# Two RWKV steps at a time: state-free products taken out of the chain, next block's preparation first

## Chip, cores and metric

The kernel runs on one core of one Trainium2 chip. The metric is the device time of one execution in microseconds; the median of several runs counts.

## The reference

One layer of a hybrid diffusion block: 512 latent tokens and 256 context tokens of width 1024. An input projection feeds two head groups. The first is bidirectional RWKV-7 time mixing with 8 heads of 64; the second is bidirectional gated linear attention in chunks of 64. Both go through one output projection, a norm, and a mixture of 16 experts (1024 to 2816 to 1024), each of which takes its best 64 tokens. All is in f32. What the change touches is the RWKV recurrence, run over context and then latent tokens in each direction:

```python
def step(s, inp):
    r_t, w_t, kk_t, kka_t, k_t, v_t = inp
    s_kk = jnp.einsum('bhvk,bhk->bhv', s, kk_t)
    s = s * w_t[:, :, None, :] - s_kk[..., None] * kka_t[:, :, None, :] + v_t[..., None] * k_t[:, :, None, :]
    y = jnp.einsum('bhvk,bhk->bhv', s, r_t)
    return s, y
```

## The kernel before

The kernel first projects the inputs in strips, then runs the gated linear attention, then the RWKV part, then the output projection, norm and routing, and last the experts, whose weights are read from HBM in one pass.

The RWKV part works in chunks of 64 tokens: 4 of context and 8 of latent tokens, so 12 chunks a direction. Each chunk is solved with a triangular inverse, so that only a 64x64 state passes from chunk to chunk. The heads are taken in four blocks b of two heads each; both directions d run in the same step, on different chunks. For each block there are these stages.

- `rw_elem` makes the decays and rates from small matrices (tiles e_c, e_w, e_i, e_t, one buffer each), and PC, the decay over a whole chunk.
- `rw_keys` writes KB (keys and removal keys, side by side) and AM (decayed removal keys). AM holds the two heads in two halves, each half zero on the other head's partitions.
- `rw_scores` (L839) multiplies KB by AM for each chunk into the score matrices SC, masked by MA.
- `rw_inverse` inverts the triangular part of SC in place: a recursion of 15 pairs of VectorE operations (L881, L884), then diagonal 32x32 products (L896, L916, L919), then the off-diagonal corrections (L931 to L946).
- `rw_rho` writes RM, the decayed receptance, with the same zero halves.
- `rw_step`, twelve times: transposes values and keys (VU, kbt); multiplies scores by values into ps_w; adds AM by state S (L981); copies to wt (L984); multiplies by the inverse (L988); copies into VU (L992); multiplies keys by VU (L1000); and updates the state, S2 = PC * (product + S), with the part PC * S made on GpSimd (L1012, L1014). For the last eight steps `rw_out` makes the outputs from RM, S, KB and VU (L1025 to L1044).
- `rw_post` normalises the block's outputs and adds bonus and gate.

`rw_prep` is scores, inverse and rho together. The loop over b issues the steps of block b, then keys and preparation of block b+1, then the elements of block b+2, then the post of block b-1. Instructions are ordered by a scheduler that takes them by program order; `H(name, b)` moves a stage ahead by the number of places that OPT gives under that name (h_crit up to 1000, h_elem 700 for block 1, h_scores 700). PSUM has eight banks: w 1, k 2, e 2, i 2, u 1; the inversion uses i, elements, scores and post use e, the steps w, k and u. A few dummy matmuls (`busy`, and at L1361) run between stages. After the last block, `rows` (L1189) adds the output projection of three quarters of the heads for row tiles 1 and 2, and `begin` (L1200) starts the accumulation for each tile, with those products inside for tiles 0 and 3.

Of the kernel before, what the change touches and what calls it, by code (L numbers as in the profile page):

```python
# [15 lines left out]
OPT = dict(h_load=-100,h_rho=(0, 500, 60, 400),rh=(1, 2, 2, 2),b1=(0, 4),h_step=(0, 0, 0, 200),adb=4,h_post=(100, -100, 0),gf=512,h_rows=(0, 100),h_acc0=-100,h_scores=(500, 700, 0, -50),h_keys=(400, 500, 0, -100),b3=(0, 8),sp=1,gse='v',ea=1,f7=3,h_glah=0,bz=(10, 10),f3=1,r0b=0,fb=3,ge=0,p2=2,p1=0,f5=1,h_elem=(0, 700, 0, 60),f2=3,b2=(4, 0),h_inv=(200, 0, 0, 100),wo=(5, 6, 3, 4, 1, 2, 0, 8, 7),f8=3,f1=2,f6=1,h_split=0,f4=1,h_sub=(60, 60, 0, 150),h_out=(300, -100, 0, -200),h_crit=(700, 1000, 100, 400),vu='aa',h_lev=(150, 0, 0, 0),pwr=0,h_kv=(0, 0, 0, 0),h_post3=150)  # L16
# [6 lines left out]
P = 128  # L23
# [13 lines left out]
def body(tc, I, out):  # L37
# [91 lines left out]
    HR = (slice(0, 64), slice(64, 128))  # L129
    smask = pcn.tile([P, TT], BF16, name="smask")  # L130
# [541 lines left out]
    KB, AM, RM, SC = [[], []], [[], []], [[], []], [[], []]  # L672
    for n in "ct":
        rpa.tile([P, 2, TT], F32, name=f"e_{n}")
    for d in range(2):
        KB[0].append(rpa.tile([P, 12, P], F32, name=f"KB0{d}"))
        AM[0].append(rpa.tile([P, 12, 2, 64], F32, name=f"AM0{d}"))

    def rw_elem_(b, pss, fill=lambda n: None):
# [10 lines left out]
        PC = zp0.tile([P, 12, 2], F32, name="PC", bufs=2)  # L690
# [43 lines left out]
    def rw_keys_(b, PC, kk, c, ws, ips, tas):  # L734
        j = b % 2
        for d in range(2):
            V.tensor_tensor(KB[j][d][:, :, VR[d]], ch(c[d]), ch(ips[d]), op=M)
            V.tensor_tensor(KB[j][d][:, :, DR[d]], ch(tas[d]), ch(ips[d]), op=M)
            for h in range(2):
                r = HR[h]  # L740
                E = (G, V)[h]
                al, k3, w3 = AM[j][d][r, :, h], ch(kk)[r], ch(ws[d])[r]
                if d == 0:
                    E.tensor_tensor(al[:, :, 1:64], k3[:, :, 1:64], w3[:, :, 0:63], op=M)
                    G.tensor_copy(al[:, :, 0], k3[:, :, 0])
                else:
                    E.tensor_tensor(al[:, :, 0:63], k3[:, :, 0:63], w3[:, :, 1:64], op=M)
                    G.tensor_copy(al[:, :, 63], k3[:, :, 63])
# [5 lines left out]
    def rw_rho_(b, pss, PC, kk, c, ws, ips, tas):  # L754
        j = b % 2
        for d in range(2):
            for h in range(2):
                r = HR[h]
                G.tensor_tensor(RM[j][d][r, :, h], ch(zr[b])[r], ch(ws[d])[r, 4:12], op=M)
# [11 lines left out]
    def clear(j):  # L771

        for d in range(2):
            for h in range(2):
                G.memset(AM[j][d][HR[1 - h], :, h], 0.0)
# [34 lines left out]
    def pu_():  # L810
        return next(puq)
# [743 lines left out]
```

## Time and profile before

| | |
|---|---|
| median of 3 runs | 2114.52 us (2105.4 to 2122.06) |
| profiled execution | 2106.32 us |
| its span, first to last instruction | 2104.6 us |
| mean granted TensorE clock | 0.961 |
| TensorE busy | 1837.8 us (87%) |
| VectorE busy | 708.1 us (34%) |
| ScalarE busy | 482.8 us (23%) |
| GpSimd busy | 309.1 us (15%) |
| DMA moved | 638.58 MB |

A share of busy time is an average over stages with different limits, and a TensorE that is busy need not be at its peak, since products in flight count in full.

### The profile page before, as it was taken

The page shows a single profiled execution, that of the slowest core. Times are in us where ns is not written, and L with a number is a line of the kernel's source. Part 1 is how long each engine was busy: PE and PEld are TensorE (multiplying, and loading weights), DVE is VectorE, ACT ScalarE, POOL GpSimd, SP SyncE. Part 2 cuts the span into 40 slices and gives each one's busy share as a digit, 9 for nine tenths or more (in the row PEclk, how much of TensorE's full clock was granted, in tenths as well). Part 3 has the DMA queues.
Part 4 walks back from the last instruction along what each step waited for, and adds up shares of the span by engine and source line. Part 5 has one row for each costly group of instructions (what it writes and reads, how often), then busy time and mean ns, then how long its engine had stood idle before and what let it go on. Part 6 is the DMA issues. An engine that isn't in the chain of part 4 may idle for free. (4 is left out here: it accounts for less than half of the span.)

```text
span 2104.6 us, 32442 instructions
## 1 busy us (share of the span) xinstructions
PE 1837.8 (87%) x13882; PEld 941.6 (45%) x13882; DVE 708.1 (34%) x1381; ACT 482.8 (23%) x984; POOL 309.1 (15%) x317
## 2 busy tenths in 40 slices
PE   5999997788889988999998988988888888889886
PEld 1776776567667653333333333333333333333322
DVE  4233668666753262123112112122122121121113
ACT  2242445555752441011101100010010010011001
POOL 2442655343230220000000000000000000000001
PEclk9999998898987999999999999999999999999998
DMA  8457631510000268999999999999999999999995
GB/s 291 139 147 219 219 106 29 174 46 18 2 28 7 87 269 367 425 424 425 425 424 424 425 425 425 424 424 425 425 425 424 424 425 424 425 425 425 424 424 224
DMA packets 135996, 638.58 MB, mean 303 GB/s; under 512 B 13007, under 2 KB 73016, under 8 KB 84908
## 3 DMA queue, kind: packets, MB, share of 16 engines
q1 hardware_dynamic: 133520, 625.74, 73.6%
q0 software_dynamic: 2016, 10.49, 1.5%
q8 instruction: 109, 1.79, 0.4%
q10 hardware_dynamic: 316, 0.28, 0.1%
q14 instruction: 35, 0.29, 0.0%
HBM read 619.54 MB, written 15.75 MB: 302 GB/s over the span
## 5 line engine op out<-in xcount | busy, mean ns | idle before, releaser
L1443 PE MATMUL ps_gu<-wt,xT 128*64 128x512 f32 (+1 forms) x3072 | 689.3, 568 | 49.6 <-DMA wt<-in_ex_up_dram 36.9
L1443 PEld LDWEIGHTS ps_gu<-wt,xT 128*64 128x64 f32 x3072 | 239.7, 138 | 436.7 <-issue 292.0
L1491 PE MATMUL ps_gu<-wd,hT 128*64 128x512 f32 x1408 | 311.2, 595 | 30.6 <-DMA wd<-in_ex_down_dram 30.6
L1491 PEld LDWEIGHTS ps_gu<-wd,hT 128*64 128x64 f32 x1408 | 97.5, 137 | 232.4 <-issue 173.7
L1464 ACT ACTIVATE gT<-ps_m 128x512 f32<-128x512 f32 x16 | 9.6, 597 | 602.7 <-PE ps_m L45 602.7
L1505 DVE TENSOR_TENSOR ye<-ps_gu,g2b 128x512 f32<-128x512 f32 x16 | 11.1, 692 | 370.9 <-PE ps_gu L1491 370.9
L1406 PE MATMUL ps_m<-h,oh 128*64 128x512 f32 x256 | 93.2, 616 | 45.6 <-DVE oh L1401 45.6
L1294 POOL MEMSET cnt<- 128x12 f32 x16 | 1.7, 108 | 885.0 <-DVE rank L1316 873.0
L296 PE MATMUL ps_d<-hh,wh 128*128 128x512 f32 (+1 forms) x336 | 126.6, 377 | 4.5 <-ACT kx L356 3.1
L1517 DVE TENSOR_TENSOR kx<-kx,ps_m 128x512 f32<-128x512 f32 x120 | 77.1, 684 | 153.9 <-PE ps_m L1511 153.9
L296 PE MATMUL ps_d<-hh,wl 128*128 128x512 f32 (+1 forms) x336 | 121.7, 362 | 5.3 <-POOL wl L288 5.3
L296 PE MATMUL ps_d<-hl,wh 128*128 128x512 f32 (+1 forms) x336 | 122.3, 364 | 2.0 <-POOL hl L267 1.9
L1408 ACT ACTIVATE xg<-ps_m 128x512 f32<-128x512 f32 x16 | 9.6, 597 | 331.6 <-PE ps_m L1406 331.6
L288 POOL TENSOR_TENSOR wl<-raw,wh 128x1024 fp32r<-128x1024 f32 x26 | 65.3, 2512 | 108.1 <-ACT wh L287 90.9
L88 DVE TENSOR_SCALAR hm<-hm 128x512 f32<-128x512 f32 (+1 forms) x48 | 19.4, 405 | 179.1 <-ACT hm L1455 179.1
L296 PEld LDWEIGHTS ps_d<-hh,wh 128*128 128x128 f32 x336 | 65.4, 195 | 20.7 <-issue 6.7
L1415 DVE TENSOR_TENSOR xT<-ps_m,mod 128x512 f32<-128x512 f32 x16 | 11.1, 692 | 188.6 <-PE ps_m L1411 188.6
L296 PEld LDWEIGHTS ps_d<-hh,wl 128*128 128x128 f32 x336 | 65.7, 195 | 14.9 <-POOL wl L288 5.5
L296 PEld LDWEIGHTS ps_d<-hl,wh 128*128 128x128 f32 x336 | 65.6, 195 | 13.5 <-POOL hl L267 3.6
L1511 PE MATMUL ps_m<-ye,gT 64*128 64x512 f32 x244 | 68.8, 640 | 0.0
L1406 PEld LDWEIGHTS ps_m<-h,oh 128*64 128x64 f32 x256 | 28.9, 142 | 85.3 <-issue 77.7
L1300 DVE SCALAR_TENSOR_TENSOR scr<-ps_m,aff,lo 128x128 bf16<-128x128 f32 (+3 forms) x60 | 33.0, 551 | 93.0 <-PE ps_m L1396 91.4
(451 smaller groups left out, 2620.8 us busy)
## 6 DMA issues: line engine op xcount, KB each, us to landing
wt<-in_ex_gate_dram SPq DMA_DIRECT2D x128, 1408.0 KB, 26.4
wt<-in_ex_up_dram SPq DMA_DIRECT2D x128, 1408.0 KB, 27.0
wd<-in_ex_down_dram SPq DMA_DIRECT2D x96, 1536.0 KB, 27.6
wd<-in_ex_down_dram SPq DMA_DIRECT2D x32, 1024.0 KB
adat<-in_ada_w_dram SPq DMA_DIRECT2D x64, 256.0 KB, 3.6
raw<-in_w_in_dram SPq DMA_DIRECT2D x25, 512.0 KB, 5.7
adat<-in_ada_w_dram SPq DMA_DIRECT2D x4, 2048.0 KB
wo_d<-wx SPq DMA_DIRECT2D x16, 512.0 KB, 3.3
```

The costliest lines, as they stand in the source:

```text
L88: V.tensor_scalar(o, o, 1.0, 2.0 ** 60, op0=A, op1=OP.min)
L288: G.tensor_tensor(wl, raw, wh.bitcast(F32), op=S_)
L296: mm(p, a[:, k, :], b[:, k, lo:lo + n], start=k + i == 0, stop=k == KD - 1 and i == 2)
L1300: V.scalar_tensor_tensor(scr[:, l:h], row[:, l:h], aff[:, t, e:e + 1], (lo if before else hi)[:, z + l:z + h], op0=OP.is_ge if before else ...
L1406: mm(p[HR[h]], oh[:, t], h2[t][:, 512 * h:512 * h + 512], start=t == 0, stop=t == 3, skip_group_check=True)
L1408: act(xg, p, AF.Copy)
L1415: V.tensor_tensor(xv, p.rearrange("p (j h s) -> p j h s", j=4, h=2), sc, op=M)
L1443: i = mm(p[HR[h]], xT[:, k], wt[:, h * FH + f0:h * FH + f0 + w], start=k == 0, stop=k == KD - 1, skip_group_check=True)
L1491: mm(py[HR[c]], hT[:, j0 + j, 64 * h:64 * h + 64], wts[h][:, j, 512 * c:512 * c + 512], start=j0 + j + h == 0, stop=j0 + j == 10 and h == ...
L1505: V.tensor_tensor(ye, py, g2b, op=M)
L1511: mm(ps_[c], gT[HR[c], t * P:(t + 1) * P], ye[HR[c]], start=not last, stop=True, skip_group_check=True)
L1517: V.tensor_tensor(x, x, ps_[c], op=A)
```

## The change

The recurrence is handled in groups of two steps. `rw_group_` makes, without the state, all that two steps need: with the inverse it forms X from the transposed AM and from scores times values; GX, the half of X that meets the state; MS, the matrix I + GX by KB (and RM plus the same for the outputs); VU; and pu, keys by VU. `rw_state_` is all that is left in the chain: MS by S is added into pu, and S2 = PC * pu. `rw_out_` makes the outputs of the two steps from VU, BS, S and MS. AM and RM lose their zero halves; the scores use one head's 64 rows for each product. The group after next is not made ahead: group g+1 is issued before the states of group g.

In the loop, keys and preparation of block b+1 are now issued before the steps of block b. All priorities but a few are set to 0, and h_crit to 300. PSUM becomes t 2, e 2, u 2 and one buffer m of two banks; the inversion shares e. The dummy matmuls are gone. `rows` projects all four row tiles, and `begin` only adds x1.

```diff
-            for h in range(2):
-                r = HR[h]
-                E = (G, V)[h]
-                al, k3, w3 = AM[j][d][r, :, h], ch(kk)[r], ch(ws[d])[r]
...
+            E = (G, V)[d]
+            al, k3, w3 = AM[j][d], ch(kk), ch(ws[d])
...
-            for c0 in range(0, 12, 4):
-                p = pe()
-                for c in range(4):
-                    mm(p[:, c * P:(c + 1) * P], KB[j][d][:, c0 + c, :], AM[j][d][:, c0 + c].rearrange("p h t -> p (h t)"),
-                       start=True, stop=True, skip_group_check=True)
-                V.tensor_tensor(SC[j][d][:, 2 * c0:2 * c0 + 8], p.rearrange("p (u t) -> p u t", t=64),
-                                MA[:, d][:, None, :].to_broadcast([P, 8, 64]), op=M)
+            for c0 in range(0, 12, 6):
+                p = [pe()[:, 0:384] for h in range(2)]
+                for c in range(6):
+                    for h in range(2):
+                        mm(p[h][:, c * 64:c * 64 + 64], KB[j][d][HR[h], c0 + c, :], AM[j][d][HR[h], c0 + c],
+                           start=True, stop=True, skip_group_check=True)
+                for h in range(2):
+                    V.tensor_tensor(SC[j][d][:, 2 * c0 + h:2 * c0 + 12:2], p[h].rearrange("p (u t) -> p u t", t=64),
+                                    MA[:, d][:, None, :].to_broadcast([P, 6, 64]), op=M)
...
-    pw_, pk_, pe, pi = (lambda t=t, n=n: bankr(t, n) for t, n in (("w", 1), ("k", 2), ("e", 2), ("i", 2)))
+    pt_, pe, pu_ = (lambda t=t: bankr(t, 2) for t in "teu")
+    pi = pe
...
+    def rw_group_(b, g):
+        j = b % 2
+        st = [(i, d, chunk(d, 2 * g + i)) for i in range(2) for d in range(2)]
+        lat = g > 1
+        VU = rc.tile([P, 2, 2, P], F32, name="VU", bufs=3)
+        pv = pt_()[:, 0:256].rearrange("p (i v) -> p i v", i=2)
+        for i, d, c in st:
+            trp(pv[VR[d], i], zv[b][:, c * 64:c * 64 + 64], ident)
+        for d in range(2):
+            act(VU[VR[d], :, d], pv[VR[d]], AF.Copy)
+        i = next(bsq)
+        BS = (rc, rc, kp2)[i].tile([P, 4, 2, 2, 64], F32, name=f"BS{i}")
+        pq = pt_()
+        for i, d, c in st:
+            tr(pq[:, (2 * i + d) * P:(2 * i + d + 1) * P], KB[j][d][:, c, :], ident)
+        act(BS[:, :, :, 0], pq.rearrange("p (q h t) -> p q h t", q=4, h=2), AF.Copy)
+        RX = rc.tile([P, 2, 2, 2, 64], F32, name="RX")
+        px = pt_().rearrange("p (i h k t) -> p i h k t", i=2, h=2, k=2)
+        for i, d, c in st:
+            trp(px[DR[d], i, :, 0], AM[j][d][:, c], ident.rearrange("p (h t) -> p h t", h=2))
+        for i, d, c in st:
+            for h in range(2):
+                mm(px[DR[d], i, h, 1], SC[j][d][VR[d], 2 * c + h, :], VU[VR[d], i, d, HC[h]], start=True, stop=True,
+                   skip_group_check=True, tile_position=(VR[d].start, DR[d].start))
+        act(RX, px, AF.Copy)
+        if lat:
+            pm = pm_()
...
+                    mm(pm[:, o:o + 64], KB[j][d][HR[h], c, :], RM[j][HR[h], d, 2 * g - 4 + i], start=True, stop=True,
+                       skip_group_check=True)
+            V.tensor_tensor(BS.rearrange("p q h k t -> p h q k t")[:, :, :, 1],
...
+        pX = pt_().rearrange("p (i h k t) -> p i h k t", i=2, h=2, k=2)
+        for i, d, c in st:
+            for h in range(2):
+                mm(pX[DR[d], i, h], SC[j][d][DR[d], 2 * c + h, :], RX[DR[d], i, h], start=True, stop=True,
+                   skip_group_check=True)
+        GX = rc.tile([P, 2, 2, 64], F32, name="GX")
+        act(GX, pX[:, :, :, 0], AF.Copy)
+        for d in range(2):
+            act(VU[DR[d], :, d].rearrange("p i (h t) -> p i h t", h=2), pX[DR[d], :, :, 1], AF.Copy)
+        MS = rc.tile([P, 2, 2, 2, 64], F32, name="MS", bufs=3)
...
+                    mm(pm[HR[h], d, i, 0:n], GX[DR[d], i, h], BS[DR[d], 2 * i + d, h, 0:n], start=True, stop=True,
+                       skip_group_check=True, tile_position=(DR[d].start, HR[h].start))
...
+        pu = pu_()[:, 0:256].rearrange("p (i d v) -> p i d v", i=2, d=2)
...
+                    mm(pu[HR[h], i, d], BS[:, 2 * i + d, h, 0], VU[:, i, d, HC[h]], start=i + d == 0, stop=2 * g + i == 0,
+                       skip_group_check=True)
+        return VU, BS, MS, pu
+
+    def rw_state_(s, S, PC, MS, pu):
+        i = s % 2
+        if S is not None:
+            for d in range(2):
+                for h in range(2):
+                    mm(pu[HR[h], i, d], MS[HR[h], d, i, 0], S[HR[h], d], start=False, stop=True, skip_group_check=True)
+        S2 = rc.tile([P, 2, 64], F32, name="S", bufs=3)
+        V.tensor_tensor(S2, pu[:, i], PC[:, s, :, None].to_broadcast([P, 2, 64]), op=M)
+        return S2
...
+    def rw_steps(b, PC):
+        def group(g):
+            with H("group", b):
+                return rw_group_(b, g)
+
+        S, nxt = None, group(0)
+        for g in range(6):
+            VU, BS, MS, pu = nxt
+            if g < 5:
+                nxt = group(g + 1)
+            Ss = []
+            for i in range(2):
+                Ss.append(S)
+                if 2 * g + i < 11:
+                    with H("crit", b):
+                        S = rw_state_(2 * g + i, S, PC, MS, pu)
+            if g > 1:
+                with H("out", b):
+                    rw_out_(b, g, Ss, VU, BS, MS)
...
     for b in range(4):
-        S = None
-        for s in range(12):
-            S = rw_step(b, s, S, PC)
+        PC0 = PC
         if b < 3:
             rw_keys(b + 1, *e)
             PC = rw_prep(b + 1, e)
+        rw_steps(b, PC0)
         if b < 2:
             e = rw_elem(b + 2, pe)
...
-    rows((1, 2))
+    rows((1, 2, 0, 3))
...
-        ps_ = (wbk, pub) if t == 2 else [(pk_, pi)[t == 0]() for c in range(2)]
+        ps_ = two(pm_()) if t in (2, 3) else [pt_() for c in range(2)]
         for c in range(2):
             mm(ps_[c], ident, x1[t][:, 512 * c:512 * c + 512], start=True, stop=False, skip_group_check=True)
-            if t in (0, 3):
-                product(ps_[c], (0, 1, 2), t, c, False, False)
```

## Rows read from the trace of the kernel before

**Rows 1.** The page, the span in 40 equal slices: GB/s moved

```profile
GB/s 291 139 147 219 219 106 29 174 46 18 2 28 7 87 269 367 425 424 425 425 424 424 425 425 425 424 424 425 425 425 424 424 425 424 425 425 425 424 424 224
```

**Rows 2.** Windows of 10 us: busy us of each engine, granted clock, DMA share, GB/s

```profile
600.00:610.00 10.00, 10.00 (x162) 7.63 (x163) 0.29 (x1) 3.72 (x10) 0.00 (x0) 0.50 0.01 3
...
700.00:710.00 10.00, 9.80 (x115) 6.10 (x113) 3.03 (x10) 3.95 (x15) 1.38 (x3) 1.00 0.46 151
...
750.00:760.00 10.00, 9.14 (x52) 6.53 (x51) 6.10 (x15) 4.59 (x11) 4.00 (x3) 1.00 1.02 399
```

**Rows 3.** Waits of the sync queue: total us, times, longest us

```profile
SPq L1217 <- PE ps_k L1037: 59.9, 1, 59.9
```

**Rows 4.** By line, one stretch each: duration min/median/max, first and last start

```profile
L839 PE MATMUL ps_e<-AM,KB x48: 272/276/582, 371.2 to 381.3; 128*128 128x128 f32 x48
...
L839 PE MATMUL ps_e<-AM,KB x48: 274/276/580, 446.3 to 457.4; 128*128 128x128 f32 x48
...
L945 ACT ACTIVATE SC<-ps_i x2: 375/482/588, 432.1 to 433.3; 32x512 f32<-32x512 f32 x1, 32x256 f32<-32x256 f32 x1
...
L945 ACT ACTIVATE SC<-ps_i x2: 374/480/587, 522.5 to 524.5; 32x512 f32<-32x512 f32 x1, 32x256 f32<-32x256 f32 x1
...
L945 ACT ACTIVATE SC<-ps_i x2: 374/480/587, 604.4 to 605.8; 32x512 f32<-32x512 f32 x1, 32x256 f32<-32x256 f32 x1
...
L945 ACT ACTIVATE SC<-ps_i x2: 375/481/587, 692.9 to 694.2; 32x512 f32<-32x512 f32 x1, 32x256 f32<-32x256 f32 x1
```

**Rows 5.** By line, 740 to 760 us: output products of the recurrence

```profile
L1037 PE MATMUL ps_k<-RM,S x12: 222/222/223, 743.6 to 746.6; 128*64 128x64 f32 x12
```

**Rows 6.** Timeline of one step of block 3: start us, us, instruction

```profile
723.80 0.45 PE L981 MATMUL ps_w<-S,AM 128*64 128x64 f32 x8
...
724.30 0.29 DVE L984 COPY wt<-ps_w 128x128 f32<-128x128 f32 x1 [1.35 <-PE ps_w L981]
...
725.35 0.44 PE L966 MATMUL ps_k<-ident,KB 128*128 128x128 f32 x2
...
726.77 0.48 DVE L1014 SCALAR_TENSOR_TENSOR S<-ps_u,PC,SP 128x64 f32<-128x64 f32 x2 [0.30 <-ACT VU L970]
```

**Rows 7.** Groups of instructions, 400 to 800 us: busy us, mean ns, idle before

```profile
L992 ACT ACTIVATE VU<-ps_u 64x128 f32<-64x128 f32 x96 | 26.0, 271 | 57.5 <-PE ps_u L988 56.1 <-DVE X L884 0.2
...
L863 ACT ACTIVATE QD<-SC 32x768 f32<-32x768 f32 x12 | 18.4, 1536 | 4.8 <-DVE SC L841 4.6
...
L968 ACT ACTIVATE kbt<-ps_k 128x256 f32<-128x256 f32 x44 | 16.7, 380 | 36.1 <-PE ps_k L966 25.7 <-PE ps_u L1000 10.2
...
L1028 DVE TENSOR_TENSOR sr<-ps_k,MR 128x256 f32<-128x256 f32 x32 | 13.5, 420 | 15.5 <-PE ps_k L1025 14.8
...
L841 DVE TENSOR_TENSOR SC<-ps_e,MA 128x512 f32<-128x512 f32 x18 | 12.3, 689 | 29.7 <-PE ps_e L839 29.5
```

**Rows 8.** L896 alone and in block 3's preparation by line; timeline around 648.6 us

```profile
L896 PE MATMUL ps_i<-t,SC x96: 182/183/211, 404.2 to 410.3; 32*32 32x16 f32 x96
...
L896 PE MATMUL ps_i<-t,SC x96: 182/209/231, 645.7 to 675.4; 32*32 32x16 f32 x96
...
648.32 0.33 PE L1037 MATMUL ps_k<-RM,S 128*64 128x64 f32 x2
648.58 0.23 PE L896 MATMUL ps_i<-zt,SC 32*32 32x16 f32 x2
648.74 0.33 PE L1037 MATMUL ps_k<-RM,S 128*64 128x64 f32 x2
```

**Rows 9.** By line, elements of block 1, then of block 2

```profile
L718 ACT ACTIVATE e_i<-e_i x2: 826/834/843, 414.5 to 427.4; 128x768 f32<-128x768 f32 x2
...
L682 ACT ACTIVATE e_c<-kx,cols x1: 935/935/935, 462.8 to 462.8; 128x768 f32<-128x768 f32 x1
...
L718 ACT ACTIVATE e_i<-e_i x2: 828/836/843, 485.3 to 506.8; 128x768 f32<-128x768 f32 x2
```

**Rows 10.** Timeline from 399 us: a run of 512-column products

```profile
399.25 2.65 PE L1091 MATMUL ps_k<-wg,mxg 128*128 128x512 f32 x11
```

More of the change, by code (lines that the diff above doesn't have):

```diff
@@ L129, in body @@
     HR = (slice(0, 64), slice(64, 128))
+    MR2 = pcn.tile([P, 4, 64], BF16, name="MR2")
+    V.tensor_copy(MR2.rearrange("p (i d) t -> p i d t", i=2), MR[:, None].to_broadcast([P, 2, 2, 64]))
+    idd = pcn.tile([P, 64], F32, name="idd")
+    for r in HR:
+        V.tensor_copy(idd[r], ident[r, r])
     smask = pcn.tile([P, TT], BF16, name="smask")
@@ L676, in body @@
         KB[0].append(rpa.tile([P, 12, P], F32, name=f"KB0{d}"))
-        AM[0].append(rpa.tile([P, 12, 2, 64], F32, name=f"AM0{d}"))
+        AM[0].append(rpa.tile([P, 12, 64], F32, name=f"AM0{d}"))
     def rw_elem_(b, pss, fill=lambda n: None):
@@ L756, in rw_rho_ @@
         for d in range(2):
-            for h in range(2):
-                r = HR[h]
-                G.tensor_tensor(RM[j][d][r, :, h], ch(zr[b])[r], ch(ws[d])[r, 4:12], op=M)
+            G.tensor_tensor(RM[j][:, d, ::1 - 2 * d], ch(zr[b]), ch(ws[d])[:, 4:12], op=M)
         khs = c[0][:, TC:TT]
@@ L769, in rw_rho @@
             return rw_rho_(b, pss, PC, kk, c, ws, ips, tas)
[L771 to L775, printed above, removed]
     until("rwr0")
-    clear(0)
     e = rw_elem(0, pss, fill)
@@ L796, in bankr, with pm_ @@
         return psr.tile([P, n], F32, name="ps_" + tag, tag=tag, bufs=bufs)
-    pw_, pk_, pe, pi = (lambda t=t, n=n: bankr(t, n) for t, n in (("w", 1), ("k", 2), ("e", 2), ("i", 2)))
-    pub = bankr("u", 1)
-    puq = itertools.cycle(pub[:, i * P:(i + 1) * P] for i in range(4))
-    wbk = pw_()
-    def busy(dep, n):
-        for _ in range(n):
-            mm(wbk[0:32, P:2 * P], dep, ident, start=True, stop=True, skip_group_check=True)
-    def pu_():
-        return next(puq)
+    pt_, pe, pu_ = (lambda t=t: bankr(t, 2) for t in "teu")
+    pi = pe
+    def pm_():
+        return psr.tile([P, 1024], F32, name="ps_m", tag="m", bufs=1)
     rp = rp2
@@ L1044, in rw_out @@
             V.tensor_tensor(o, o, p3, op=A)
-    def rw_step(b, s, S, PC):
-        with H("step", b):
-            return rw_step_(b, s, S, PC)
+    def rw_steps(b, PC):
[8 more added lines that the diff above has]
+            Ss = []
+            for i in range(2):
+                Ss.append(S)
+                if 2 * g + i < 11:
+                    with H("crit", b):
[3 more added lines that the diff above has]
+                    rw_out_(b, g, Ss, VU, BS, MS)
     def rw_post(b, parts=((0, 4, 1),)):
@@ L1321, in body @@
     lo, hi, _ = masks(op_)
-    h2 = [kp2.tile([P, D], F32, name=f"h2{i}", tag=n) for i, n in enumerate(("RM00", "RM01", "gt", "t2"))]
+    h2 = [kp2.tile([P, D], F32, name=f"h2{n}", tag=n) for n in ("RM0", "BS2", "gt", "t2")]
     for part in ((1, 2), (0, 3)):
@@ L1354, in body @@
             if t == 1:
-                row0 = O("r0b", 0) and pe() or pw_()
+                row0 = pu_()
                 cnt0 = ranks(op_, 0, row0, True)
@@ L1360, in body @@
             if t == 3:
-                for n, d in zip(O("bz",(0,20)), (hT[:, 0, 0:32], lgs[:, 0:32])):
-                    for _ in range(n):
-                        mm(pub[0:32, 0:P], d, ident, start=True, stop=True, skip_group_check=True)
                 rank0 = cnt0[1]()
```

145 lines of the change are left out of this document (40 added, 105 removed).

## Prediction

> **What bounds the kernel now.** I read the page's 40 slices first. From the 17th slice on, the transfers run at 424 to 425 GB/s and stay there to the end [rows 1]: the experts' weights stream at a fixed rate. A ten-us window at 750 us already moves 399 GB/s [rows 2], so the stream starts there. The change touches no line of the experts' loop, so the span is "when the stream starts" plus a constant. What starts it? The sync queue's own waits show one of 59.9 us, for the matmuls of L1037, the output products of the recurrence [rows 3]: until the last recurrence step is out, the memory that the loads behind it need is in use. So a us off the recurrence's end is a us off the span.
>
> The second question is what paces the recurrence between 371 and 747 us. It consists of four blocks of two heads. For each there is a preparation (scores L839, then the inversion of the triangular matrices, whose last copies are L945) and twelve steps. The inversions of blocks 0 to 3 end at 433, 525, 606 and 694 us [rows 4]. Block 3's steps come after 694 and end with the output products L1037, the last of which starts at 746.6 [rows 5]; the other blocks' steps lie in the same way behind their own inversion. So the steps of three of the four blocks lie beside the next block's preparation, and **the preparations, not the steps, set the pace** there: 91, 81 and 88 us from one inversion's end to the next. Only block 3's steps stand alone, 53 us from 694 to 747.
>
> One preparation has run with no step beside it: block 0's, 371.2 to 433.3, or 62 us, though with 512-column products of the gated-attention half in the same stretch [rows 4]. Block 1's ran from 446.3 to 524.5 [rows 4]; with steps beside it a preparation took 78 us. Some 16 us are thus interference, and more in block 3. Where it comes from is visible in the diagonal products L896: alone they take 6 us (404.2 to 410.3), in block 3's preparation 30 us (645.7 to 675.4), cut into pairs that alternate with pairs of step products [rows 8].
>
> **The change, part by part.**
>
> *The chain of a step.* Today it is: products with the state (L981), a copy (L984), products with the inverse (L988), two ACT copies (L992), products with the keys (L1000), two DVE updates (L1014): 3.45 us from 723.80 to the end of S at 727.25 [rows 6]. Afterwards it is four products with the state and one DVE operation on 128x128. For these I take 0.45 (a bound from above, since that row holds eight products) and 0.29 us (L984 has that shape), with 0.2 for two hand-overs, four times the 0.05 from L981 to L984: 0.9 us. Eleven of them are 10 us. The chain stops being a limit of anything.
>
> *The work that is taken out of the chain* doesn't vanish. Per group of two steps ACT copies four tiles of 64x256, one of 128x256 and two of 128x512. The rows show 0.27 us for 128 columns and 0.38 for 256 [rows 7], so my estimate for 512 is 0.6; 5 x 0.38 + 2 x 0.6 = 3.1 us a group, 18.6 us a block. Before, it was four copies of 0.27 and one of 0.38 a step, 1.46 x 12 = 17.5 us: equal. DVE has per late group 0.69 (128x512, L841), twice 0.42 (L1028) [rows 7] and twice 0.29 = 2.1 us; before, 0.29 + 0.48 + 0.42 a step, 2.4 for two: equal. POOL loses the product SP. TensorE gets more: a block had 64 products of 128 columns and 256 of 64; it gets 152 and 256. A 128-column product costs at most 0.22 us (L966, two in 0.44), an overlapped one of 64 columns 0.056 (L981, eight in 0.45) [rows 6]; most of the 88 new ones fill half the array or less and overlap in the same way, so they add 5 to 19 us a block, and I take 7. It lies where TensorE waits: the four copies L863 of 1.54 us [rows 7] and the DVE recursion behind them, some 17 us a block. Without that cover it is 7 us a block, 28 in all; this is why I don't take the preparation at its best value below.
>
> *Zero halves dropped.* The scores become 48 half-height products in place of 24 full ones, and the mask moves from six operations of 512 columns to eight of 384, about 0.55 us each (between 0.42 and 0.69): 4.1 against 4.4 us. But a round now holds both banks, so products and masks no longer alternate: +2 us on each preparation (0 to 4). Clears and half-height key products on POOL go, off the path: 0.
>
> *Next block first, and the priorities gone.* Keys, scores and inversion of block b+1 now precede the steps of block b in program order. They issue no transfer; what they are moved past on DVE, ACT, POOL and TensorE are the steps. The offsets that lifted the steps' critical instructions by up to 1000 places become 300, for five short instructions a step. So the preparation should come near its undisturbed 62 us. A step's instruction already running still blocks it, and the 2 us above are added: **I take 66 us**, between 62 and the 78 of block 1 (block 3 took longer). The steps get the rest: 18.6 us of ACT and about 30 of TensorE (below) a block fit beside it.
>
> *Elements of the next block but one (rw_elem).* Block 1's lose their lift of 700 and share two PSUM banks with the inversion, since pi is now pe. Their last exponent came at 427.4 [rows 9]; the keys, held by the gated half, follow at 436, so 8 us of slack cover a delay. I take +5 us (0 to 23, the upper end if they run wholly after 433). Block 2's began at 462.8, without a lift already, and the last exponent came at 506.8 [rows 9]: its keys can be ready when the inversion of block 1 ends, give or take 4 us, which I put on each later period.
>
> *The end.* Block 3's six groups: a late group has 76 products, 76 x 0.056 = 4.3 us, and some fifteen changes of form at about 0.1 more each [rows 8], so 5.8 us; an early one about 3.5; together 30. The output projection's products, some 40 of which lie between 694 and 747, cost 0.23 us each in a run (eleven in 2.65 us, the last with its latency) [rows 10]: 9 us. So **40 us against 53**, with 32 (none of them in the way) and 50 (a group waits for its copies as well) as bounds. Afterwards all four row tiles are projected before the first norm, two more than today: four DVE adds of 0.69 us and up to 36 products (8 us) stand earlier in the queue; gaps take most. +3 us (0 to 8). The dummy matmuls ahead of the first expert go; the stream runs by then, so 0.
>
> **The sum.** First period: 433.3 to 436 for the gated half, +5, 10 for the keys (436 to 446.3, where the scores start [rows 4]), +66 = 84 against 91: -7. Second and third: 66 + 4 = 70 against 81 and 88: -11 and -18. Last block -13, end +3: **-46 us**. The profiled execution took 2106.3 us (span 2104.6), so 2060; it lies 8 us under the median of the three runs shown, 2114.5, and I add half of that: **2064 us**.
>
> **A rule against the change.** A change between forms of product costs time: around 648.6 us pairs of 32x32 and 128x64 products alternate, and each pair begins 0.16 to 0.26 us after the last [rows 8], where eight of one form take 0.45 together [rows 6]. The Trainium skill, TensorEngine Tiling (Array Packing), section Key Properties, says that changing the tiling mode, not just the tile, drains the engine; the rows agree. By that rule, steps in four forms that fill the gaps of an inversion in a fifth are its worst neighbours; rival 1 is its result here.
>
> **The rivals.**
>
> *1. The inversion stays interleaved.* For: block 3's L896 took 24 us longer than alone, by alternation; a scheduler that fills each gap with a ready step product can do the same again. Against: the inversion now goes first, so its 192 ready products should come out in one run. Price: periods as today, block 3 -13, end +3, elements +5: -5, or 2105 by the same half offset, within 1%. Chance 0.16.
>
> *2. The preparation runs free, and keys and scores overlap the tail of the previous inversion.* Then a period is 57 us. With the first at 84 - 8 that is 190 against 261, -71; block 3 at 34 us, -19; end 0: 2106 - 90 + 4 = 2020. Against: the elements of block b+2 need keys(b+1) to be through and took 44 us [rows 9], so the loop of 44 + 10 us has almost no room for a delay. Chance 0.13.
>
> *3. Slower: the elements become the gate.* They are now last in order, behind the steps, and share banks with the inversion. If for blocks 2 and 3 they run only behind the inversion, a period is 66 + 44 + 10 = 120 in place of 81 and 88, +71 for the two; first period -7, block 3 -13, end +3: 2106 + 54 + 4 = 2164. It turns into a loss from a period of 93 us, that is, when the elements end 17 us after the inversion beside them, and passes 1% at 27 us. For: shared banks, no priority. Against: block 2's had no lift and ended 18 us before the inversion. Chance 0.10.
>
> **How the numbers follow.** Forecast 0.61, rival 1 0.16, rival 2 0.13, rival 3 0.10. About 1% (21 us) is what a measurement of this kernel can tell from no change; the three runs span 2105 to 2122. The forecast's own bounds: preparations of 62 and an end of 32 us give 2043; 75, 50 and +8 give 2105. Under 2093 lie rival 2, most of the forecast (0.54) and 0.01 of rival 1: 0.68. Within 1%: 0.07 + 0.15 = 0.22. Slower: 0.10. The range leaves out half of rival 2 and rival 3: 2020 to 2112.
>
> **What would show it.** Right: inversions ending near 517, 587 and 657; L896 in under 10 us per block; block 3's steps in 40 us; the expert stream at full rate from about 704. Wrong: periods of 80 us and more with L896 in pairs (rival 1); ACT and DVE idle before the keys of blocks 2 and 3 while elements finish (rival 3). The granted clock was 1.00 at 700 to 710, beside block 3's steps, and 0.50, which is 1.2 GHz, at 600 to 610, with the inversion's end alone [rows 2]; if inversions without steps beside them stay at the lower level, 66 us will not be reached.

## The result, and the profile after

The changed kernel takes 2202.85 us (median of 4 runs, 2194.31 to 2205.53) against 2109.96 for the kernel before in the same comparison: a ratio of 1.0426 [1.0367, 1.0484]. The forecast was 2064 with a range to 2112. The profiled execution took 2204.24 us, its span is 2202.1.

The page of the changed kernel, slices of the span: granted clock in tenths and GB/s.

```profile
PEclk9999998868755698899999999999999999999998
...
GB/s 285 142 163 211 190 108 86 110 14 8 11 12 15 3 88 257 321 425 424 425 424 425 425 424 425 425 425 425 425 425 424 425 425 424 424 425 424 425 426 235
```

The stream reaches its full rate from the 18th slice where it was the 17th [rows 1], and keeps it. So the first step of the prediction holds: the loss lies ahead of the stream. By line, the ends of the four inversions, then the end of block 3's outputs, in the changed kernel:

```profile
L929 ACT ACTIVATE SC<-ps_e x2: 374/481/588, 435.2 to 436.2; 32x512 f32<-32x512 f32 x1, 32x256 f32<-32x256 f32 x1
...
L929 ACT ACTIVATE SC<-ps_e x2: 374/480/587, 521.0 to 522.4; 32x512 f32<-32x512 f32 x1, 32x256 f32<-32x256 f32 x1
...
L929 ACT ACTIVATE SC<-ps_e x2: 374/480/587, 627.0 to 628.4; 32x512 f32<-32x512 f32 x1, 32x256 f32<-32x256 f32 x1
...
L929 ACT ACTIVATE SC<-ps_e x2: 374/480/587, 752.3 to 753.6; 32x512 f32<-32x512 f32 x1, 32x256 f32<-32x256 f32 x1
...
L1025 PE MATMUL ps_t<-MS,S x64: 218/242/268, 803.5 to 829.0; 64*64 64x64 f32 x64
```

Against [rows 4, 5] the first inversion is 3 us later; the periods (from one inversion's end to the next) are 86, 106 and 125 us where they were 91, 81 and 88; block 3's steps take 75 us after the inversion where they took 52; and from there to the end of the span, the tail, are 1373 us where there were 1358. The loss of 97.5 us between the two spans is +3 -5 +25 +37 +23 +15, in that order.

What grew inside the periods is seen from where the scores begin (by line: blocks 2 and 3 in the kernel before, then blocks 1, 2 and 3 in the changed kernel):

```profile
L839 PE MATMUL ps_e<-AM,KB x44: 275/276/581, 524.6 to 537.8; 128*128 128x128 f32 x44
...
L839 PE MATMUL ps_e<-AM,KB x46: 274/276/580, 607.8 to 621.0; 128*128 128x128 f32 x46
```

```profile
L824 PE MATMUL ps_e<-AM,KB x96: 272/369/473, 454.0 to 476.7; 64*128 64x64 f32 x96
...
L824 PE MATMUL ps_e<-AM,KB x96: 272/417/472, 558.7 to 581.8; 64*128 64x64 f32 x96
...
L824 PE MATMUL ps_e<-AM,KB x96: 271/369/474, 679.0 to 701.9; 64*128 64x64 f32 x96
```

A preparation of blocks 1 to 3, from the scores to the end of the inversion, took 79, 82 and 87 us and takes 69, 70 and 75 now. But in the kernel before, the scores of blocks 2 and 3, all but a few early records, began about when the inversion ahead of them ended (525 and 607 us); now they begin 36 and 50 us after it. The preparations became shorter; the waits ahead of them grew by more.

Where the elements went (by line: first operation of blocks 2 and 3, last exponents of each):

```profile
L687 ACT ACTIVATE e_c<-kx,cols x2: 937/937/937, 525.1 to 631.1; 128x768 f32<-128x768 f32 x2
...
L722 ACT ACTIVATE e_w<-e_i x2: 835/836/836, 550.4 to 566.9; 128x768 f32<-128x768 f32 x2
...
L722 ACT ACTIVATE e_w<-e_i x2: 831/837/843, 668.3 to 685.0; 128x768 f32<-128x768 f32 x2
```

Block 2's ran from 463 to 507 beside the inversion of block 1 [rows 9]. Now they begin 2 us after that inversion has ended and are over at 568, and the keys, scores and next inversion come behind. Windows in their stretch show what this leaves TensorE (columns as in [rows 2]; PE is the first pair, the clock stands behind POOL):

```profile
545.00:555.00 10.00, 2.24 (x5) 0.85 (x4) 7.61 (x8) 9.41 (x16) 5.05 (x4) 0.60 0.00 0
...
665.00:675.00 10.00, 2.93 (x4) 0.79 (x3) 8.31 (x6) 7.87 (x12) 6.51 (x3) 0.50 0.00 0
```

TensorE works 2 to 3 us of 10, beside ACT and DVE at work on elements, and the granted clock is 0.60 and 0.50; 0.50 is its 1.2 GHz level.

Windows over the whole stretch from the first inversion's end to the steps' end, kernel before, then changed kernel:

```profile
435.00:754.00 319.00, 286.60 (x4738) 212.08 (x4736) 173.07 (x392) 159.54 (x392) 95.75 (x122) 0.88 0.11 32
```

```profile
435.00:830.00 395.00, 346.49 (x5435) 267.44 (x5434) 168.56 (x322) 182.24 (x335) 54.61 (x57) 0.72 0.07 22
```

The engine is busy 90% and 88% of it. Busy time by clock is 286.6 x 0.88 = 252 and 346.5 x 0.72 = 249 us: a rough sum, since products in flight count in full, but it says that the stretch holds about as much work at full clock as before. The stretch of before also holds 51 of the 96 records of the output projection, where that of the changed kernel holds none, so the changed recurrence is the heavier one; and it is done at a lower clock.

### The profile page after: what moved, and what is told of

It is laid out like the page before. It is cut to its first block, busy times and chain, and to the rows that moved or that the text cites. A ratio compares the mean times of both kernels' runs of the same rounds, so it can differ in the third digit from the quotient of the medians.

```text
span 2202.1 us, 33601 instructions
## 1 busy us (share of the span) xinstructions
PE 1929.2 (88%) x14602; PEld 1015.4 (46%) x14602; DVE 704.8 (32%) x1320; ACT 490.8 (22%) x908; POOL 256.4 (12%) x241
## 5 line engine op out<-in xcount | busy, mean ns | idle before, releaser
L1438 PE MATMUL ps_gu<-wt,xT 128*64 128x512 f32 (+1 forms) x3072 | 703.4, 576 | 49.1 <-DMA wt<-in_ex_up_dram 35.7
L1401 PE MATMUL ps_m<-h2RM,oh 128*64 128x512 f32 x64 | 42.9, 791 | 48.1 <-DVE oh L1396 48.1
L824 PE MATMUL ps_e<-AM,KB 64*128 64x64 f32 x384 | 53.4, 360 | 21.8 <-ACT e_t L89 16.5
L824 PEld LDWEIGHTS ps_e<-AM,KB 64*128 64x128 f32 x384 | 50.2, 266 | 27.6 <-issue 21.1
```

What stands on the lines that cost most here:

```text
L824: mm(p[h][:, c * 64:c * 64 + 64], KB[j][d][HR[h], c0 + c, :], AM[j][d][HR[h], c0 + c], start=True, stop=True, skip_group_check=True)
L1401: mm(p[HR[h]], oh[:, t], h2[t][:, 512 * h:512 * h + 512], start=t == 0, stop=t == 3, skip_group_check=True)
L1438: i = mm(p[HR[h]], xT[:, k], wt[:, h * FH + f0:h * FH + f0 + w], start=k == 0, stop=k == KD - 1, skip_group_check=True)
```

## The experiments

All ratios are to the kernel before, measured beside each run, with 95% intervals; the changed kernel has 1.0426 [1.0367, 1.0484]. Differences in us are between medians of different comparisons, in which the kernel before took 2110 to 2119; against the changed kernel, the ratios put them up to 8 us lower. The intervals of a2_rho, a11_half and, just, a9_tail overlap that of the changed kernel, so their gains are not certain.

**Priorities.** The kernel before with the changed kernel's values of OPT (`h_...` 0, `h_crit=300`).

> The kernel before with the priorities of the changed kernel (h_crit 300, h_load -100, h_post3 150, all others 0); order, banks, steps and dummy products as before. If losing the priorities is what costs (the elements of block 1 lose 700 places): 40 us or more above the kernel before, 2150 and up. If the new steps cost: within 15 us of the kernel before.

2120.53 us, ratio 0.9999 [0.9976, 1.0023]. In the kernel before, with its order and banks, losing the priorities costs nothing; what they would do in the changed kernel was not tried.

**The loop turned**, alone in the kernel before:

```diff
-        S = None
-        for s in range(12):
-            S = rw_step(b, s, S, PC)
+        PC0 = PC
         if b < 3:
             rw_keys(b + 1, *e)
             PC = rw_prep(b + 1, e)
+        S = None
+        for s in range(12):
+            S = rw_step(b, s, S, PC0)
...
```

(PC gets a third buffer as well.)

> The kernel before with only the loop turned: keys and preparation of block b+1 are issued ahead of the steps of block b; steps, banks, priorities and dummy products as before. Theory A: the elements of block 3 still lie behind the steps in program order, as before, so within 15 us of the kernel before. My forecast's own idea (the preparation comes nearer its undisturbed 62 us): 15 to 40 us faster. If the turn itself is at fault: 20 us or more slower.

2208.81 us, ratio 1.0419 [1.0388, 1.0451]. By the copies of its steps (L984, blocks 0 and 1), the first ran at 504.8 us, when the next inversion (last copies at 511.7) was nearly over; in the kernel before, block 0's first ran at 439:

```profile
L984 DVE COPY wt<-ps_w x24: 290/292/293, 504.8 to 683.2; 128x128 f32<-128x128 f32 x24
```

The dummy matmuls of the inversion write the steps' bank, and now stand ahead of the steps. So again without them (`b1`, `b2`, `b3` to 0):

> The kernel before with the loop turned (next block's preparation first), and without the dummy matmuls of the inversion, which write the bank of the steps. Theory: in e2_first it was these dummies, now ahead of the steps in the order of the program, that held every step to the next inversion's end; without them the steps run beside the inversion again, and the time is within 25 us of before (2095 to 2145). Rival: the turned order itself (the steps come after the next block's work on every engine's list) costs the 90 us; then it stays at 2190 to 2215.

2168.81 us, 1.0241 [1.0207, 1.0274]: the dummies made 40 us of it, and neither theory's number came. The remaining 53 us come with the turn, unless the lack of the dummies itself costs something. Then the turn undone in the changed kernel, `rw_steps(b, PC)` ahead of the keys:

> The changed kernel with the loop in its old order: the groups of a block are issued ahead of the next block's keys, scores and inversion. Theory D (turned order: the steps of block b come last on TensorE, so they end late, and the keys of block b+2, which write the same buffers, wait for them; e2b_first_nd showed 53 us of this in the kernel before): the steps of blocks 0 to 2 end some 20 us earlier each, 2140 to 2175. Rival (load of the groups): the preparation is late by what the steps gain, 2190 to 2215.

2239.11 us, 1.0580 [1.0547, 1.0613], 36 us slower than with the turn. Both theories fall: beside the new groups the turn is a gain. The scores of block 1, which take 23 us with the turn, ran from 454.1 to 520.3, cut up by groups.

**Elements issued ahead of the block's steps**, the other edits kept:

> The changed kernel, with the elements of block b+2 issued in program order ahead of the steps of block b, not behind them; nothing else. Theory A (the elements are the gate: in the changed kernel those of blocks 2 and 3 start only when the steps beside them are out, at 543 and 657 us): they now start right after the keys of the block before, so the second and third period lose 25 to 35 us each, and the time falls by 45 to 70 us, to 2130 to 2160. Theory B (TensorE is full: every f32 product is two records there, so a late group of 76 products takes near 10 us at full clock and more at half): the elements only take gaps that the steps then miss, and the time falls by less than 20 us, above 2180.

2228.15 us, 1.0508 [1.0465, 1.0552]. The elements still began at 522.0 and 643.7, 3 to 4 us behind the inversions' ends. Their place in the program was not what held them.

**The shared pair of banks**, alone in the kernel before:

```diff
+    pi = pe
```

> The kernel before with one line more: the inversion takes its banks from the pair that scores, elements and rho use, as the changed kernel does. Theory C (shared banks): rho of a block, next in line for a bank behind the inversion's products, waits for the inversion's end, gives back e_c only then, and the elements of the block after run behind the inversion with TensorE idle; 40 to 90 us slower than before, about 2170, elements L706 of block 2 after 525 us where they began before the inversion's end. Rival (TensorE's load in the groups and the lost dummies make the time): the pair of banks costs little, within 15 us of before.

2191.57 us, 1.0352 [1.0298, 1.0406]: 75 us from one line. By line in that kernel, the last copies of block 1's inversion and the exponents of block 2, which come after it as in the changed kernel:

```profile
L946 ACT ACTIVATE SC<-ps_e x2: 375/482/588, 533.0 to 534.2; 32x512 f32<-32x512 f32 x1, 32x256 f32<-32x256 f32 x1
...
L718 ACT ACTIVATE e_i<-e_i x2: 831/834/837, 550.4 to 572.1; 128x768 f32<-128x768 f32 x2
```

Rho stands behind the inversion in the program, takes its bank after the inversion's products, and frees e_c; the elements need e_c. The pattern of the changed kernel is there from this line alone: later periods of 109 and 118 us, and a tail of 1373 us. The same in the changed kernel, from the other side: rho ahead of the inversion (`rh=(1, 1, 1, 1)`).

> The changed kernel with rho of blocks 1 to 3 placed ahead of the inversion and not behind it. Theory C (shared banks): rho gets its bank before the inversion's products, e_c comes free some 80 us earlier, the elements of the next block run beside the inversion, the stretches of half clock with ACT and DVE alone go: 2145 to 2170. Rival (load of the groups on TensorE): the elements move but the time stays within 15 us of the changed kernel's 2203.

2193.85 us, 1.0356 [1.0319, 1.0393]: -9 us, not -40. The elements' first operation came early (480.7), but their first products came only at 533.3, 13 us after the inversion that holds the shared pair, among the groups on TensorE, and L711 at 544.7. So elements and rho on the groups' pair `pt_`:

> The changed kernel with the products of the elements and of rho in the groups' pair of banks and not in the pair of the inversion. Theory C: elements and rho no longer wait for the inversion: 2120 to 2165, the elements of blocks 2 and 3 over before the inversion of the block ahead of them ends. Rival (load): they move, the time stays at 2190 to 2210; a third way is that they now wait for the groups in their new pair, which would show as a gap before L687 that ends with the copies of a group.

2221.14 us, 1.0502 [1.0453, 1.0550]: it fits the third way, though the gap lies behind L687. L687 came at 466.4, the products for L711 (554.9) only after the groups' products in the pair. So rho and then the elements between scores and inversion:

```diff
         if r == 1:
             rw_rho(b, pe, *e)
+        if b in (1, 2):
+            e2.append(rw_elem(b + 1, pe))
         rw_inverse(b)
...
-            e = rw_elem(b + 2, pe)
+            e = e2[b]
```

> The changed kernel with rho of every block ahead of its inversion, and the elements of blocks 2 and 3 issued between this rho and the inversion of the block ahead of them, so that they have the shared pair of banks before the inversion does. Theory C (shared banks): the elements are over before that inversion ends, keys wait only for the steps' buffers: 2150 to 2180, against 2194 for a2_rho, where rho alone was moved. Rival: the inversion now waits for the elements' copies in the shared pair by as much as they gain, or the keys wait for the steps anyway: 2185 to 2205.

2203.31 us, 1.0423 [1.0377, 1.0469]. Now block 2's elements are over at 509 us, 58 earlier than in the changed kernel, and nothing is gained. The timeline of TensorE there:

```profile
491.96 0.80 PE L710 MATMUL ps_e<-LS,e_ws 96*128 96x512 f32 x1 [2.79 <-ACT e_t L712]
501.42 0.70 PE L991 MATMUL ps_m<-BS,GX 64*64 64x64 f32 x14 [8.66 <-ACT GX L982]
```

It waits 8.66 us for a copy of the group, which stands in ACT's queue behind the elements; the groups of block 0 slip, their last state comes at 561 in place of 539, and the keys of block 2, which write the buffers that these groups read, begin no earlier. POOL's write of AM shows which wait ends last, changed kernel, then a8_early:

```profile
550.56 2.58 POOL L719 TENSOR_TENSOR e_c<-e_c,kx 128x768 f32<-128x768 f32 x1 [4.56 <-ACT e_c L718]
553.11 2.18 POOL L747 TENSOR_TENSOR AM<-e_c,e_w 128x756 f32<-128x756 f32 x1
```

```profile
553.28 2.60 POOL L747 TENSOR_TENSOR AM<-e_c,e_w 128x756 f32<-128x756 f32 x1 [48.47 <-PE ps_t L45]
```

In the changed kernel it follows the elements; with these out of the way it waits for block 0's transposes (L45), the groups' reading of AM. So the second gate opened when the first had, and the scores still begin 32 and 41 us after the inversions. Last, elements, rho and post on a bank of their own, taken from the groups (`("t", 1), ("e", 2), ("u", 2), ("x", 1)`), and that with the outputs ordered as below:

> The changed kernel with the elements, rho and post on a bank of their own, which the groups give up (they keep one bank for their transposes and products where they had two); the output products of the first half go to the pair of the states. Theory C (the pair shared with the inversion makes elements, rho and post late; in the kernel before the same sharing cost 75 us): 2140 to 2180 against 2203, the elements of block 2 before the end of the inversion of block 1, post of block 2 and with it the output products before the end of block 3's inversion. Rival (what a8_early showed: the group's copies wait behind the elements on ACT, TensorE idles and its clock falls), with the groups' single bank on top: 2195 to 2225.

> a15_own with the outputs ordered by form, as a10_fixout, which gained 32 us. If the clock and the banks were two separate losses: 20 to 32 us below a15_own, under theory C then 2110 to 2160; if the rival holds, 2165 to 2195.

2237.32 us, 1.0555 [1.0518, 1.0592], and 2202.93, 1.0404 [1.0364, 1.0443], both above the ranges of theory and rival. It is the rival's way, only more so: with one bank, TensorE waits in a15_own for each copy of a group (waits of TensorE, 430 to 830 us), and block 2's elements end at 539 us, 23 behind the inversion of block 1, so they were not set free:

```profile
PE ps_t L980 <- ACT RX L966: 10.4, 13, 3.2
PE ps_t L45 <- ACT BS L957: 8.5, 13, 1.2
PE ps_m L992 <- ACT GX L983: 6.0, 10, 1.3
```

One thing came back: from the last output to the end are 1361 us in both, for 1373 in the changed kernel; the post of block 2 no longer comes behind block 3's inversion (below).

**The outputs by form.** `rw_out_` alternates products of VU (128 rows) and of the state (64 rows), four records at a time.

```diff
-        for d in range(2):
-            for i in range(2):
+        for k in range(2):
+            for d in range(2):
+                for i in range(2):
...
-                for k in range(2):
```

> The changed kernel, with the 16 output products of a group ordered by form: first the eight with VU and BS (128 rows), then the eight with S and MS (64 rows), in place of turns of two. Six changes of form less in each of 16 groups, 96 in all. Theory B (TensorE is full, and changes of form cost 0.1 us at 2.4 GHz and 0.2 at 1.2): 10 to 20 us of TensorE go, most of them on the path, 2182 to 2195. Theory A (elements gate): what TensorE does in the steps decides only in block 3, so 2 to 4 us, 2197 to 2202.

2173.88 us, 1.0249 [1.0212, 1.0287]. In this kernel the sums of the outputs change; a10_fixout starts each half bank once (`start=k + d + i == 0`), and they are those of the changed kernel.

> The changed kernel with the eight products of VU of an output ahead of the eight of the state, so that TensorE changes its tile form once and not sixteen times a group; each half bank is started once, by its first product. Theory: as a3_out, which gained 29 us, 2165 to 2185. Rival (the gain of a3_out came from its changed accumulation): within 8 us of 2203.

2170.81 us, 1.0252 [1.0233, 1.0272]: -32 us. (By the code the changes of form fall from seven a group to one, not from the expectation's sixteen.) Timelines of TensorE, changed kernel at half clock and a10_fixout at full clock:

```profile
654.03 0.48 PE L1025 MATMUL ps_t<-BS,VU 128*64 128x64 f32 x4
654.44 0.48 PE L1025 MATMUL ps_t<-MS,S 64*64 64x64 f32 x4
654.85 0.48 PE L1025 MATMUL ps_t<-BS,VU 128*64 128x64 f32 x4
```

```profile
795.85 0.69 PE L1025 MATMUL ps_t<-BS,VU 128*64 128x64 f32 x16
```

Four records in turn take 0.41 us from start to start at half clock and 0.26 at full (806.53, 806.79, 807.06 in the changed kernel); sixteen of one form take 0.69 together. The 32 us are more than the turns, for which the expectation of a3_out had 10 to 20: over 620 to 690 us the clock was 0.50 in the changed kernel and 0.68 here (windows, TensorE alone; changed kernel, then a10_fixout).

```profile
620.00:690.00 70.00, 60.45 (x542) 0.50 0.03 9
```

```profile
620.00:690.00 70.00, 58.49 (x664) 0.68 0.07 20
```

**The tail.** The output products of blocks 0 to 2 issued ahead of the last post (`rows((1, 2, 0, 3))` before `rw_post(3, ...)`):

> The changed kernel with the output products of blocks 0 to 2 issued ahead of the last post and not behind it (both take their banks from the shared pair, and they began 2 us after the last post's product, at 831.8 us, when the steps were over). Theory C: the 96 products run between the groups of block 3 and beside its inversion, as they did before the change, and the tail is 10 to 30 us shorter: 2175 to 2195. Rival: they push the groups of block 3 back by the same, and the time stays within 8 us of 2203.

2188.41 us, 1.0345 [1.0317, 1.0372], the number of the theory, but not its mechanism: all but two of the 96 records still ran after the last output, and the tail is 1373 us as in the changed kernel. The 14 us came in the third period (106 us for 125), again with a clock of 0.69 over 620 to 690. In the changed kernel the splits and weight loads of these products come at 786 to 795 us (by line), where they came from 686 in the kernel before:

```profile
L1177 ACT ACTIVATE mx<-ym x3: 621/622/630, 786.3 to 787.9; 128x512 fp32r<-128x512 f32 x3
...
L1170 POOL DMA_DIRECT2D w<-wo_d x8: 535/567/591, 787.1 to 794.5; - x8
```

They follow the post of block 2, which takes banks from the shared pair and so comes behind block 3's inversion, which ends at 754.

**The scores by halves**, alone in the kernel before: the products of the changed kernel, on AM with its zero halves in place.

> The kernel before with the scores alone taken from the change: two products of 64 rows and 64 columns for each product of 128 by 128, their zero halves dropped, 96 of TensorE's records a block for 48. Theory S (a record costs 0.11 us at full clock and 0.21 at half, whether its tile is whole or a quarter, so dropping the zero halves doubles the scores): 15 to 40 us slower than before. Rival (the inversion of another block and the steps fill the time, or the quarter tiles overlap): within 10 us of before.

2160.83 us, 1.0224 [1.0187, 1.0261]: +46 us, more than theory S said. Its first inversion alone ends 16 us later (450 us). Runs of score records from the changed kernel's timeline, one at full clock and two at half:

```profile
367.77 1.17 PE L824 MATMUL ps_e<-AM,KB 64*128 64x64 f32 x18
...
558.65 2.82 PE L824 MATMUL ps_e<-AM,KB 64*128 64x64 f32 x24 [8.23 <-ACT e_t L89]
...
562.45 2.82 PE L824 MATMUL ps_e<-AM,KB 64*128 64x64 f32 x12
```

Block 2's scores take 23 us for 96 records, where 48 took 10 to 13 in the kernel before; some 11 of the 23 are three gaps of 1.4, 3.2 and 6.9 us, in which TensorE runs products of groups. Theory S's size holds for part of the records alone. From start to start a record of 64 rows takes 0.11 us at full clock and 0.21 at half, as one of 128x128 does in the kernel before; but in the 18 and the 24 the two heads' records fall side by side and a pair takes that together, in the 12 none do. Then one product of 128 rows for two in the changed kernel, which adds the two heads' scores up, alone (a11_half), behind three edits with lower times (a12_four), and those three without it (a13_three):

> The changed kernel with one score product of 128 rows by 64 columns where it has two of 64 rows; both heads read the same sum, so the scores, and all that follows from them, are not the reference's. Theory S: 48 records a block for 96, 8 to 10 us less in each of three periods: 2165 to 2185. Rival (the scores wait on the keys and the copies anyway): 2195 to 2205.

> The changed kernel with three edits that each gained alone: outputs ordered by form (32 us), rho ahead of the inversion (9), output products ahead of the last post (14). If the gains are separate 2140 to 2155; if rho's and the tail's were only a shorter stretch of half clock in the third period, which the order of the outputs shortens as well, 2160 to 2175.

> a13_three with the single score product of a11_half; the scores are not the reference's. If scores, outputs, rho and tail are the whole loss, 2105 to 2130, no slower than before; if the load of the groups and the lost overlap of elements and inversion still cost 40 us or more, 2145 to 2165.

2188.15 us (1.0344 [1.0295, 1.0393]), 2163.66 (1.0230 [1.0200, 1.0261]) and 2173.22 (1.0265 [1.0221, 1.0309]), in that order. Gains of 32, 14 and 9 us alone are 39 together and not 55: in a13_three, too, the clock over 620 to 690 is higher (0.74), and that can be gained only once. Taking half the score products out of it gains nothing (10 us more). In the changed kernel the scores of blocks 1 and 2 wait for the elements anyway, ahead of their first products (waits of TensorE, 430 to 830 us):

```profile
PE ps_e L824 <- ACT e_t L89: 16.5, 2, 8.2
```

No kernel with the new steps beats the kernel before; a13_three has the lowest time of them.

## Why the prediction was wrong

*The stream and the constant behind the recurrence*: right. The span grew by what the recurrence took, and by 15 us of tail. The term for the end, +3 (0 to 8), was mis-sized: it counted work moved, not that post of block 2 would wait for the pair of banks that the inversion of block 3 holds. a15_own and a16_own_out give 12 of the 15 back, and e3_bank, where the kernel before got the shared pair and nothing else, has the changed kernel's 1373 us.

*The chain of a step*: the form was right. Products with the state take 0.45 us and S 0.29, with waits 1.3 us from 815.56 in place of 3.45 [rows 6]; what paces block 3 is the groups (timeline of the changed kernel, steps of two groups and one S):

```profile
805.90 0.45 PE L1010 MATMUL ps_u<-S,MS 64*64 64x64 f32 x8
...
807.68 0.45 PE L1010 MATMUL ps_u<-S,MS 64*64 64x64 f32 x8
...
815.56 0.45 PE L1010 MATMUL ps_u<-S,MS 64*64 64x64 f32 x8
...
816.58 0.29 DVE L1012 TENSOR_TENSOR S<-ps_u,PC 128x128 f32<-128x128 f32 x1 [1.26 <-PE ps_t L1025]
```

*Cost of a group on TensorE*: the first step that failed in size. I read "eight in 0.45" [rows 6] as eight products at 0.056 us. A step has four products there: each is two records, as [rows 4] shows with 48 records for 24 products of scores. A late group's 76 products are 148 records (its four transposes of KB are one each), and take 9.7 us at full clock (805.90 to 815.56), not 5.8. Block 3 took 75 us and not 40, and of these 24 are not its own: the groups of block 2 were still to be done when block 3's inversion ended, which I left out. Block 2's last state, then block 3's first, by DVE's timeline:

```profile
774.02 0.29 DVE L1012 TENSOR_TENSOR S<-ps_u,PC 128x128 f32<-128x128 f32 x1
...
784.93 0.29 DVE L1012 TENSOR_TENSOR S<-ps_u,PC 128x128 f32<-128x128 f32 x1 [0.71 <-PE ps_u L1001]
```

From 778, when block 2's outputs are out, block 3 takes 51 us.

*Zero halves dropped*, +2 (0 to 4) on each preparation: mis-sized. Twice the records are twice the time where the heads' halves don't fall side by side; the scores take some 10 us more a block, gaps included, and the part alone cost the kernel before 46 us. In the changed kernel it costs little: -15 us without it (a11_half), not clear of the noise. There the first inversion ends 13 us earlier, the second period is 11 us longer and the third 17 shorter. That the waits for the elements hide the rest is argued, not shown.

*Next block first*: the term was nearly right. Interleaving did go (rival 1 fell: block 3's diagonal products, L881 in the changed kernel, ran in 4.3 us, 725.8 to 730.1, for 30 before), preparations took 69, 70 and 75 us against the 66 forecast, and the turn gains 36 us in the changed kernel. What failed is "the steps get the rest": the groups of blocks 0, 1 and 2 did not fit beside the inversions, and their last states came 16, 25 and 20 us after these had ended.

*Elements, "its keys can be ready when the inversion of block 1 ends, give or take 4 us"*: the step that failed most. In place of 4 us the scores of blocks 2 and 3 began 36 and 50 us after the inversion ahead of them; these 78 us are over half of the 143 between the forecast's -46 and the measured +97.5. I weighed the priorities and kept the elements' start; what moved them was the line `pi = pe`, whose chain (inversion, rho, e_c, elements) I had in the diff and did not follow. And I never asked when the keys may write: KB and AM have two buffers, and in the new order the groups that read them end after the inversion. a8_early shows this second gate behind the first. The late elements are rival 3, with a chance of 0.10 and 2164 us: its periods of 120 us became 106 and 125. Its price of 2164 counts block 3 at -13 and no tail beyond +3; with the measured +23 and +15 it is 2212, near the 2203 measured.

*The clock*: named in the last sentence as what would spoil the 66 us, without a price. Much of the lost time is seen there: 0.72 for 0.88 over the recurrence.

*What is shown and what is not.* Shown: the pair of banks alone costs 75 us, the scores by halves alone 46, in the kernel before; the turns of form cost 32 in the changed one, some of it through the clock; and the waits ahead of the scores are the largest part of the miss, with the groups as a second gate behind the elements. Not shown: how the 93 us divide in the changed kernel, and that it would gain with both gates gone; no run removes both. The parts don't add. Where the elements were set free (a8_early), the groups lost as much, on ACT. Giving the inversion a pair of its own while the groups keep theirs was not tried: the kernel's tiles take all eight banks, and a bank of the states (u) or of m in place of the groups' was not given up. That the low clock follows from TensorE's idle stretches is read from the windows, not tested by itself.

**A rule.** The turns agree with the Trainium skill, TensorEngine Tiling (Array Packing), section Key Properties, by which a change of tiling mode drains the engine: 0.26 us for four records in turn where sixteen of one form take 0.69. I had looked for its harm in the gaps of the inversion; it sat inside `rw_out_`.

## What to carry to other kernels

Follow a shared bank or buffer through everything that stands between its users in the program: one line of it moved a 45 us stage off its cover. When the order of two stages is turned, ask anew who still reads the buffers that the next one writes. Count how many records a product is before dividing a row's time by products, and ask what drops in number, not in columns, when zero halves go. Where stages compete for one engine with a variable clock, single gains don't add: test the sum.

## What was not expected of the hardware

- Products of two heads on the two halves of the array's rows ran side by side only at times, in the same stretch and form: a pair of records in 0.11 us at full clock, or one record in 0.11 (a pair or one in 0.21 at half clock).
- Small edits moved the granted clock over 620 to 690 us from 0.50 to between 0.65 and 0.74, in a10_fixout, a9_tail, a2_rho, a11_half and a13_three, with TensorE about as busy (56 to 59 us of 70, for 60); the third period went from 125 to between 104 and 109 us. Which way the cause runs was not tested.
